# A chunked delta rule on TensorE: products of the next chunk issued in turn with those of this one

## The chip, the cores and the metric

The kernel runs on one core of a Trainium2 chip. The metric is the device time of one execution in microseconds (us). Before the change the median of three runs is 3013.03 us (3005.29 to 3014.2).

Matrix products run on TensorE (PE in the profile), elementwise work on VectorE (DVE) and ScalarE (ACT), which also empty the banks that TensorE writes. TensorE works its instructions off in the order in which the program lists them.

## What is computed

A trunk of two layers over 1024 tokens of width 1024. In each layer two kinds of recurrent heads run beside each other, then a gated feed-forward block and a gated embedding add. The change lies in the odd layer, in the heads of the delta rule, 8 heads of 64 by 64 state each:

```python
def step(state, xs):                                   # _rwkv7_scan, one token
    r_t, w_t, k_t, v_t, kk_t, a_t = xs
    sa = jnp.einsum("bhij,bhj->bhi", state, -kk_t)
    state = (state * w_t[:, :, None, :] + sa[..., None] * (kk_t * a_t)[:, :, None, :]
             + v_t[..., None] * k_t[:, :, None, :])
    return state, jnp.einsum("bhij,bhj->bhi", state, r_t)
```

The kernel does not step token by token. It takes 64 tokens (a chunk) at once, with one triangular inverse for each head and chunk, and only the state goes from chunk to chunk.

## The kernel before

**Two kinds of work share TensorE.** The dense products (all projections, feed-forward and gates) write banks named `acc`: each weight block and each operand is split into a high and a low part (`whi`, `wlo`, `xhi`, `xlo`, `ghi`, `glo`), and three products of 512 columns replace one. There are some 10,700 of them. The mixers' products write banks named `mx`, drawn by `bank()` from a pool of four. They are plain float32, and the profile counts each of them as two passes (transposes as one). A scheduler that sees a number for each instruction (`at`, `tick`, `lagging`) puts the mixers' products between the dense ones, so that dense products fill the time in which a mixer waits for ScalarE or VectorE.

**The delta rule.** `r7_unit` works on 256 tokens, four times in all (u = 0 to 3), each with four chunks of 64 (c = 0 to 3). In order:

- The two small projections (`lora` in the names): rows 0 to 63 of the array for the first, 64 to 127 for the second, four banks, emptied by ScalarE.
- `r7_scores`, for all four chunks: products of `ar` and `bk` for the even heads on rows 0 to 63, for the odd heads on rows 64 to 127, a bank each. VectorE masks each bank into `pm`.
- `r7_inverse`: a triangular inverse on VectorE and some 32 by 32 products; its result is `tt`.
- `r7_chunk`, chunk after chunk. Per chunk: four transposes of `bk` (L199), copied by ScalarE into `bt` (L1041); four products of `v` with the constant `cen`, the **values**, on columns 0 to 63 of the array, copied into the low half of `vu` (L1046); one bank that takes, for each pair of heads in turn, a product of the state `r_S` with `ar` (the **received** part, 128 rows by columns 64 to 127) and two products of `pm` with the values (the **open** part, 64 rows by 64 columns), copied into `r` (L1057); eight products of `tt` with `r` (the **solved** part, rows and columns 64 to 127), copied into the high half of `vu` (L1063); one bank for the output, again in turn one state product on the full array and two of `pm` with `vu` on column halves, copied into `o` (`keepC`, L1070); eight products of `bt` with `vu` on alternate column halves, from which VectorE makes the new state.

A row such as `128*64` in the profile gives the rows and columns of the array that a product uses. In the names `w` stands for `vu`, `r` or `bt`, which share a pool, and `sm` for `v`.

Of the kernel before, what the change touches and what calls it, by code (L numbers as in the profile page):

```python
# [10 lines left out]
F32 = mybir.dt.float32  # L11
# [8 lines left out]
P = 128  # L20
# [7 lines left out]
W2 = 7  # L28
# [80 lines left out]
class Trunk:  # L109
# [82 lines left out]
    def mm(self, out, lhsT, rhs, start=True, stop=True):  # L192
        with self.lagging():
            self.nc.tensor.matmul(out, lhsT, rhs, start=start, stop=stop)  # L194
        self.tick()

# [726 lines left out]
    def r7_unit(self, z, u, mixed):  # L923
        nc = self.nc
# [11 lines left out]
        for rows, bias, dst in ((slice(0, 64), self.w0h, w1), (slice(64, P), self.a0h, ta)):  # L936
            for jj in range(2):
                ps = self.bank()
                for j in (2 * jj, 2 * jj + 1):
                    self.mm(ps[:, UNIT * (j % 2):UNIT * (j % 2 + 1)], self.lora[rows, P * j:P * j + P], wag[rows, 0])  # L940
                for j in (2 * jj, 2 * jj + 1):
                    self.act(dst[:, j], ps[:, UNIT * (j % 2):UNIT * (j % 2 + 1)], AF.Tanh,
                             bias=bias[:, j:j + 1], scale=0.5)
# [77 lines left out]
    def r7_scores(self, c, ar, bk):  # L1021
        C = 64
        pm = self.work.tile([P, 2, 4, P], F32, tag="w4", bufs=W4, name=self.name("pm"))
        for par in range(2):
            rows = slice(C * par, C * par + C)
            ps = self.bank()
            for j in range(4):
                self.mm(ps[:, P * j:P * j + P], bk[rows, j, c], ar[rows, j, c])
            self.mul(pm[:, par], ps.rearrange("p (j t) -> p j t", j=4),
                     self.rmask.unsqueeze(1).broadcast_to([P, 4, P]))  # L1030
        return pm

    def r7_chunk(self, c, ar, bk, v, gs, o, pm, tinv, first):

        nc = self.nc
# [5 lines left out]
        nc.scalar.copy(bt, ps.rearrange("p (j t) -> p j t", j=4))  # L1041
        vu = self.work.tile([P, 8, C], F32, tag="w2", bufs=W2, name=self.name("w2_"))
        ps = self.bank()
        for j in range(4):
            self.mm(ps[0:C, P * j:P * j + P], v[:, j, C * c:C * c + C], self.cen)
        nc.scalar.copy(vu[0:C], ps[0:C].rearrange("p (h e) -> p h e", h=8))  # L1046
        hi = slice(C, P)
        S = self.r7_S[self.r7_i]
        ps = self.bank()
        for j in range(4):  # L1050
            if not first:
                self.mm(ps[hi, P * j:P * j + P], ar[:, j, c, 0], S[:, j], True, False)
            for par in range(2):
                h = 2 * j + par
                self.mm(ps[hi, C * h:C * h + C], pm[0:C, par, j, 0:C], vu[0:C, h], first, first or par == 1)
        r = self.work.tile([P, 8, C], F32, tag="w2", bufs=W2, name=self.name("w2_"))
        nc.scalar.copy(r[hi], ps[hi].rearrange("p (h e) -> p h e", h=8))  # L1057
        ps = self.bank()
        for j in range(4):
            for par in range(2):  # L1060
                h = 2 * j + par
                self.mm(ps[hi, C * h:C * h + C], tinv[:, 4 * par + j], r[hi, h])
        nc.scalar.copy(vu[hi], ps[hi].rearrange("p (h e) -> p h e", h=8))  # L1063
        ps = self.bank()
        for j in range(4):
            if not first:
                self.mm(ps[:, C * j:C * j + C], S[:, j], ar[:, j, c, 1], True, False)
            for par in range(2):
                self.mm(ps[C * par:C * par + C, C * j:C * j + C], vu[:, 2 * j + par], pm[:, par, j, C:P], first, True)
        nc.scalar.copy(o[:, :, C * c:C * c + C], ps[:, 0:4 * C].rearrange("p (j t) -> p j t", j=4))  # L1070
        ps = self.bank()
        for j in range(4):
            for par in range(2):
                self.mm(ps[C * par:C * par + C, C * j:C * j + C], bt[:, j, C * par:C * par + C], vu[:, 2 * j + par])
        pv = ps[:, 0:4 * C].rearrange("p (j e) -> p j e", j=4)
        self.r7_i ^= 1
        S2 = self.r7_S[self.r7_i]
        t = self.work.tile([P, 4, C], F32, tag="w1", bufs=2, name=self.name("w1_"))
        for par in range(2):
            rows = slice(C * par, C * par + C)  # L1080
            self.add(t[rows], pv[rows], S[rows, :, rows])
            self.mul(S2[rows, :, rows], t[rows], gs[rows, :, c:c + 1].broadcast_to([C, 4, C]))

# [403 lines left out]
```

## Time and profile before

| | |
|---|---|
| median of the runs | 3013.03 us |
| the profiled execution | 3014.3 us |
| its span, first to last instruction | 3012.6 us |
| PE busy | 2937.0 us, 97% |
| DVE busy | 1958.8 us, 65% |
| ACT busy | 1253.9 us, 42% |
| DMA, mean rate | 119 GB/s |

Matrix products are pipelined: one lasts longer than the distance to the next. What a product costs is read from the distance between the starts of neighbouring rows, not from its duration.

### The profile page before, as it was taken

How to read it: one execution, taken by the hardware profiler on the slowest of the kernel's cores; microseconds unless marked ns; L12 is line 12 of the kernel's file. 1: busy time of each engine (PE TensorE's matmuls, PEld its weight loads, DVE VectorE, ACT ScalarE, POOL GpSimd, SP SyncE). 2: the span in 40 equal slices, each digit the busy share in tenths (PEclk: the TensorE clock that was granted, in tenths of full speed). 3: DMA queues.
4: the chain of work that ended last, by engine and by line, in shares of the span. 5: the costliest groups of instructions: out<-in, count | busy, mean ns of one | idle time of the engine just before them, and what ended most of it. 6: DMA issues, size and time to landing. Idle time of an engine off the chain costs nothing.

```text
span 3012.6 us, 38754 instructions
## 1 busy us (share of the span) xinstructions
PE 2937.0 (97%) x15102; PEld 2381.2 (79%) x15102; DVE 1958.8 (65%) x3313; ACT 1253.9 (42%) x1783; POOL 28.0 (1%) x97
## 2 busy tenths in 40 slices
PE   8999989999999999999999999999999999999997
PEld 6877768878878887877877778787878777888886
DVE  7566655756687557836787584684787497555457
ACT  5354554333244536224444443542453454322224
POOL 0000010000000000000000000000000000000000
PEclk9999989999999999999999999999999999999999
DMA  5443553333245554422333444532333135333333
GB/s 198 143 156 104 186 200 98 107 88 105 81 118 168 168 166 128 104 66 91 102 102 102 133 141 143 161 95 67 91 116 98 51 96 170 98 119 98 98 91 105
DMA packets 197287, 357.79 MB, mean 119 GB/s; under 512 B 64848, under 2 KB 100816, under 8 KB 197104
## 3 DMA queue, kind: packets, MB, share of 16 engines
q1 hardware_dynamic: 197104, 355.33, 38.7%
q8 instruction: 118, 1.93, 0.3%
q14 instruction: 65, 0.53, 0.1%
HBM read 298.61 MB, written 56.66 MB: 118 GB/s over the span
## 4 chain that ended last, share of the span: by engine, by line
PE 84%; DVE 9%; ACT 3%; issue 2%; DMA 1%; POOL 0%; SPq 0%; DVEq 0%; ACTq 0%; POOLq 0%
PE acc L194 71%; PE mx L194 13%; DVE wlo L168 2%; DVE w L181 1%; DVE w L168 1%; DVE tmp L168 1%; PE mx L199 1%; ACT w L189 1%; ACT whi L332 1%; DVE cols L168 1%; ACT L189 0%; DVE h L181 0%; DVE tmp L181 0%; DVE w L789 0%; DMA h<-in_x_dram 0%
## 5 line engine op out<-in xcount | busy, mean ns | idle before, releaser
L194 PE MATMUL acc<-xhi,whi 128*128 128x512 f32 x2864 | 1140.5, 399 | 11.8 <-ACT whi L332 8.8
L194 PE MATMUL acc<-xlo,whi 128*128 128x512 f32 x2864 | 1131.3, 396 | 4.2 <-DVE xlo L168 3.3
L194 PE MATMUL acc<-xhi,wlo 128*128 128x512 f32 x2864 | 1128.1, 394 | 2.7 <-DVE wlo L168 2.6
L332 ACT CAST whi<-wraw 128x1024 fp32r<-128x1024 f32 (+1 forms) x450 | 463.6, 1030 | 1158.9 <-PE acc L194 834.8
L194 PEld LDWEIGHTS acc<-xhi,whi 128*128 128x128 f32 x2864 | 540.2, 189 | 132.1 <-ACT whi L332 9.8
L194 PEld LDWEIGHTS acc<-xlo,whi 128*128 128x128 f32 x2864 | 540.1, 189 | 123.5 <-DVE xlo L168 7.2
L194 PEld LDWEIGHTS acc<-xhi,wlo 128*128 128x128 f32 x2864 | 539.4, 188 | 123.8 <-DVE wlo L168 6.0
L168 DVE TENSOR_TENSOR wlo<-wraw,whi 128x1024 fp32r<-128x1024 f32 (+1 forms) x450 | 539.0, 1198 | 102.8 <-ACT whi L332 101.7
L168 DVE TENSOR_TENSOR tmp<-acc,rs 128x512 f32<-128x512 f32 (+1 forms) x205 | 140.8, 689 | 354.4 <-PE acc L194 354.0
L194 PE MATMUL acc<-ghi,whi 128*128 128x512 f32 x704 | 277.6, 396 | 1.0 <-ACT ghi L332 1.0
L194 PE MATMUL acc<-glo,whi 128*128 128x512 f32 x704 | 275.0, 391 | 0.0
L194 PE MATMUL acc<-ghi,wlo 128*128 128x512 f32 x704 | 275.0, 391 | 0.0
L168 DVE TENSOR_TENSOR tmp<-tmp,acc 128x512 f32<-128x512 f32 x88 | 60.4, 686 | 166.1 <-PE acc L194 165.7
L189 ACT ACTIVATE w<-w 128x1024 f32<-128x1024 f32 (+2 forms) x124 | 113.3, 920 | 113.0 <-DVE w L168 53.3
L194 PEld LDWEIGHTS acc<-ghi,whi 128*128 128x128 f32 x704 | 131.9, 188 | 29.8 <-ACT ghi L332 1.9
L194 PEld LDWEIGHTS acc<-ghi,wlo 128*128 128x128 f32 x704 | 132.1, 188 | 27.9 <-issue 0.3
L194 PEld LDWEIGHTS acc<-glo,whi 128*128 128x128 f32 x704 | 132.2, 188 | 27.2 <-DVE glo L168 0.6
L181 DVE SCALAR_TENSOR_TENSOR h<-acc,h 128x512 f32<-128x512 f32 x144 | 98.7, 687 | 63.0 <-PE acc L194 62.4
L189 ACT ACT_TABLE_LOAD x84 | 107.8, 1283 | 10.3 <-DMA h<-in_x_dram 4.7
L181 DVE SCALAR_TENSOR_TENSOR tmp<-tmp,tmp 128x512 f32<-128x512 f32 x120 | 82.2, 686 | 12.7 <-ACT tmp L189 12.6
L189 ACT ACTIVATE tmp<-tmp 128x512 f32<-128x512 f32 x120 | 75.4, 629 | 28.9 <-DVE tmp L168 28.0
L181 DVE SCALAR_TENSOR_TENSOR w<-zin,cols,w 128x256 f32<-128x256 f32 x192 | 82.5, 479 | 5.5 <-ACT w L189 5.2
(296 smaller groups left out, 2603.8 us busy)
## 6 DMA issues: line engine op xcount, KB each, us to landing
wraw<-in_ffn_w_gate_dram SPq DMA_DIRECT2D x88, 512.0 KB, 3.6
wraw<-in_ffn_w_up_dram SPq DMA_DIRECT2D x88, 512.0 KB, 3.6
wraw<-in_ffn_w_down_dram SPq DMA_DIRECT2D x64, 512.0 KB, 3.6
wraw<-in_o_w_in_dram SPq DMA_DIRECT2D x60, 512.0 KB, 3.6
wraw<-in_e_w_in_dram SPq DMA_DIRECT2D x48, 512.0 KB, 3.7
wraw<-in_ple_w_gate_dram SPq DMA_DIRECT2D x32, 512.0 KB, 3.7
wraw<-in_ffn_w_down_dram SPq DMA_DIRECT2D x32, 384.0 KB, 3.1
up<-tmp SPq DMA_DIRECT2D x32, 256.0 KB, 2.3
```

The lines of the kernel that those rows point to most:

```text
L168: (eng or self.nc.vector).tensor_tensor(out, a, b, op=op)
L181: self.nc.vector.scalar_tensor_tensor(out, a, s, b, op0=op0, op1=op1)
L189: self.nc.scalar.activation(out, a, f, **kw)
L194: self.nc.tensor.matmul(out, lhsT, rhs, start=start, stop=stop)
L199: self.nc.tensor.transpose(out, a, self.ident)
L332: self.nc.scalar.copy(hi, src)
```

## The change

Nothing is added to or taken from the computation: both programs have the same 15,102 passes on TensorE. What changes is their order and which of them share a bank.

- `together` runs several lists of products side by side, one product of each in turn, and keeps that order on TensorE.
- The two small projections and the scores are issued with the two row halves in turn.
- The values and the open part of a chunk no longer stand in that chunk. Those of chunk 0 are issued ahead of the loop; those of chunk c + 1 are issued inside chunk c. The values of c + 1 (columns 0 to 63) go in turn with the received part of c (columns 64 to 127), the open part of c + 1 (rows 0 to 63) in turn with the solved part of c (rows 64 to 127).
- The open part starts the bank; the received part of the next chunk adds to it and ends it. That bank is held meanwhile.
- In the output bank the four state products come first, then the eight of `pm`.

```diff
+    def together(self, *products):
+        with self.tc.manual_schedule(engines={mybir.EngineType.PE}):
+            for _ in zip_longest(*products):
+                pass
...
+        vu = self.vu()
+        self.together(self.r7_values(0, v, vu))
+        ps = self.bank()
+        self.together(self.r7_open(ps, pms[0], vu, u == 0))
         for c in range(4):
             tc = tinv[c // 2][64:P, 8 * (c % 2):8 * (c % 2) + 8]
-            self.r7_chunk(c, ar, bk, v, gs, o, pms[c], tc, u == 0 and c == 0)
+            ps, vu = self.r7_chunk(c, ar, bk, v, gs, o, pms, tc, ps, vu, u == 0 and c == 0)
...
+    def r7_values(self, c, v, vu):
+        C = 64
         ps = self.bank()
         for j in range(4):
-            self.tr(ps[:, P * j:P * j + P], bk[:, j, c].rearrange("p i t -> p (i t)"))
+            self.mm(ps[0:C, P * j:P * j + P], v[:, j, C * c:C * c + C], self.cen)
+            yield
+        self.nc.scalar.copy(vu[0:C], ps[0:C].rearrange("p (h e) -> p h e", h=8))
+
+    def r7_open(self, ps, pm, vu, alone=False):
+        C = 64
+        for h in range(8):
+            j, par = divmod(h, 2)
+            self.mm(ps[C:P, C * h:C * h + C], pm[0:C, par, j, 0:C], vu[0:C, h], h == 0, alone and h == 7)
+            yield
...
-        for j in range(4):
-            if not first:
-                self.mm(ps[hi, P * j:P * j + P], ar[:, j, c, 0], S[:, j], True, False)
-            for par in range(2):
-                h = 2 * j + par
-                self.mm(ps[hi, C * h:C * h + C], pm[0:C, par, j, 0:C], vu[0:C, h], first, first or par == 1)
...
+        def received():
+            for j in range(4):
+                if not first:
+                    self.mm(ps[hi, P * j:P * j + P], ar[:, j, c, 0], S[:, j], False, j == 3)
+                yield
+            nc.scalar.copy(r[hi], ps[hi].rearrange("p (h e) -> p h e", h=8))
+        self.together(received(), *(() if last else (self.r7_values(c + 1, v, nvu),)))
+
+        def solved(sums):
+            for h, (j, par) in enumerate(heads):
+                self.mm(sums[hi, C * h:C * h + C], tinv[:, 4 * par + j], r[hi, h])
+                yield
+            nc.scalar.copy(vu[hi], sums[hi].rearrange("p (h e) -> p h e", h=8))
+        sums = self.bank()
+        nps = None if last else self.bank()
+        self.together(*(() if last else (self.r7_open(nps, pms[c + 1], nvu),)), solved(sums))
+        sums = self.bank()
+        if not first:
+            for j in range(4):
+                self.mm(sums[:, C * j:C * j + C], S[:, j], ar[:, j, c, 1], j == 0, False)
+        for h, (j, par) in enumerate(heads):
+            self.mm(sums[C * par:C * par + C, C * j:C * j + C], vu[:, h], pm[:, par, j, C:P], first and j == 0, j == 3)
```

**First place: TensorE, unit u = 2, chunk 0, from the received part to the solved part.** Before (`mx_15466` is the bank that received and open part share, `w_2710` is `vu`):

```order
L194 MATMUL mx_15466<-w_2710_15459,pm_15228 64x64 x2
L194 MATMUL mx_15466<-r_S_9213,ar_15096 64x128
L194 MATMUL mx_15466<-w_2710_15459,pm_15228 64x64 x2
L194 MATMUL acc_17857<-xhi_17232,whi_17853 128x512
L194 MATMUL acc_17857<-xlo_17233,whi_17853 128x512
L194 MATMUL acc_17857<-xhi_17232,wlo_17854 128x512
L194 MATMUL acc_17857<-xhi_17236,whi_17853 128x512
L194 MATMUL mx_15481<-w_2713_15479,tt_15370 64x64 x8
```

After, the same place (the received part fills `mx_15522`, the values of chunk 1 fill `mx_15546`; `mx_15558` is chunk 1's open part, `mx_15557` chunk 0's solved part):

```order
L194 MATMUL mx_15522<-r_S_9213,ar_15156 64x128
L194 MATMUL mx_15546<-cen,sm_15250 64x128
L194 MATMUL acc_17977<-xlo_17353,whi_17973 128x512
L194 MATMUL acc_17977<-xhi_17352,wlo_17974 128x512
L194 MATMUL acc_17977<-xhi_17356,whi_17973 128x512
L194 MATMUL acc_17977<-xlo_17357,whi_17973 128x512
L194 MATMUL acc_17977<-xhi_17356,wlo_17974 128x512
L194 MATMUL mx_15558<-w_2714_15542,pm_15301 64x64
L194 MATMUL mx_15557<-w_2713_15541,tt_15430 64x64
```

The first two rows are the last of four such pairs, the last two the first of eight. The group in which state and `pm` products took turns is gone; its halves stand beside the values and the solved part of another chunk.

**Second place: TensorE, the same chunk, the output bank.** Before (`mx_15491`):

```order
L194 MATMUL mx_15491<-pm_15228,w_2710_15459 64x64 x2
L194 MATMUL mx_15491<-ar_15096,r_S_9213 128x64
L194 MATMUL mx_15491<-pm_15228,w_2710_15459 64x64 x2
L194 MATMUL mx_15505<-w_2710_15459,w_2709_15457 64x64 x8
L199 MATMUL mx_15519<-ident,bk_15097 128x128 x4
```

After (`mx_15579`):

```order
L194 MATMUL mx_15579<-ar_15156,r_S_9213 128x64 x4
L194 MATMUL acc_17977<-xhi_17360,whi_17973 128x512
L194 MATMUL mx_15579<-pm_15288,w_2708_15512 64x64 x8
L194 MATMUL mx_15593<-w_2708_15512,w_2712_15539 64x64 x8
L205 MATMUL mx_15607<-ident,bk_15157 128x128 x4
```

The four state products moved into one row ahead of the eight others.

**Third place: ScalarE, the copies of the same chunk.** Before (values, received and open, solved, output):

```order
L1046 COPY w_2710_15459<-mx_15460 64x512
L1057 COPY w_2713_15479<-mx_15466 64x512
L1063 COPY w_2710_15459<-mx_15481 64x512
L1070 COPY keepC_15226<-mx_15491 128x4x64
L1041 COPY w_2719_15524<-mx_15519 128x512
```

After (received and open, values of chunk 1, solved, output, next transposes):

```order
L1089 COPY w_2713_15541<-mx_15522 64x512
L1057 COPY w_2714_15542<-mx_15546 64x512
L1096 COPY w_2708_15512<-mx_15557 64x512
L1106 COPY keepC_15286<-mx_15579 128x4x64
L1079 COPY w_2722_15612<-mx_15607 128x512
```

The copy of the values now follows right behind that of the received part, and the pair of open and solved products stands behind both.

## Rows read from the trace of the kernel before

**Rows 1.** The page: engines' busy time, granted clock, chain by engine

```profile
PE 2937.0 (97%) x15102; PEld 2381.2 (79%) x15102; DVE 1958.8 (65%) x3313; ACT 1253.9 (42%) x1783; POOL 28.0 (1%) x97
...
PE 84%; DVE 9%; ACT 3%; issue 2%; DMA 1%; POOL 0%; SPq 0%; DVEq 0%; ACTq 0%; POOLq 0%
```

**Rows 2.** Busy time by stretch: length, PE, PEld, DVE, ACT, POOL, clock, DMA, GB/s

```profile
2066.00:2124.00 58.00, 58.00 (x479) 42.27 (x476) 14.51 (x25) 18.21 (x29) 0.68 (x3) 1.00 0.10 29
...
2404.00:2497.00 93.00, 86.64 (x458) 71.62 (x456) 84.36 (x129) 50.72 (x65) 0.00 (x0) 0.98 0.39 126
```

**Rows 3.** Timeline, TensorE, u = 2, chunk 0: start, length, form, passes

```profile
2067.25 0.76 PE L194 MATMUL mx<-cen,sm 128*64 128x128 f32 x5
2067.74 0.32 PE L194 MATMUL mx<-r_S,ar 128*64 128x128 f32 x1
2067.84 0.27 PE L194 MATMUL mx<-cen,sm 128*64 128x128 f32 x1
...
2068.26 0.50 PE L194 MATMUL acc<-xhi,whi 128*128 128x512 f32 x1
...
2069.16 0.44 PE L194 MATMUL mx<-w,pm 64*64 64x64 f32 x4
...
2071.36 0.44 PE L194 MATMUL mx<-w,pm 64*64 64x64 f32 x4
2071.73 0.50 PE L194 MATMUL acc<-xhi,whi 128*128 128x512 f32 x1
2072.07 0.40 PE L194 MATMUL acc<-xlo,whi 128*128 128x512 f32 x1
...
2072.53 0.40 PE L194 MATMUL acc<-xhi,whi 128*128 128x512 f32 x1
2072.86 1.14 PE L194 MATMUL mx<-w,tt 64*64 64x64 f32 x16
2073.93 0.43 PE L194 MATMUL mx<-ar,r_S 128*128 128x64 f32 x2
...
2075.32 0.43 PE L194 MATMUL mx<-ar,r_S 128*128 128x64 f32 x2
2075.68 0.34 PE L194 MATMUL mx<-pm,w 128*64 128x64 f32 x4
...
2076.94 0.34 PE L194 MATMUL mx<-pm,w 128*64 128x64 f32 x4
2077.11 0.64 PE L194 MATMUL mx<-w,w 128*64 128x64 f32 x16
2077.68 0.66 PE L199 MATMUL mx<-ident,bk 128*128 128x128 f32 x4
```

**Rows 4.** Timeline, TensorE: full-array products of 64 columns in one row

```profile
2436.82 1.89 PE L194 MATMUL mx<-w 128*128 128x64 f32 x16
2438.53 0.48 PE L194 MATMUL acc<-xhi,wlo 128*128 128x512 f32 x1
```

**Rows 5.** Timeline, TensorE: small projections of u = 0 and of u = 1

```profile
1126.86 2.96 PE L194 MATMUL mx<-sm,lora 64*128 64x256 f32 x16
1130.28 0.50 PE L194 MATMUL acc<-xhi,whi 128*128 128x512 f32 x1 [0.46 <-ACT xhi L332]
...
1506.70 2.00 PE L194 MATMUL mx<-sm,lora 64*128 64x256 f32 x12
```

**Rows 6.** Timeline, TensorE and VectorE: scores of u = 1 and their masking

```profile
1563.16 5.04 PE L194 MATMUL mx<-ar,bk 64*128 64x128 f32 x64
...
1564.35 4.88 DVE L168 TENSOR_TENSOR pm<-mx,rmask 128x512 f32<-128x512 f32 x8 [1.05 <-PE mx L194]
```

**Rows 7.** Timeline, ScalarE and VectorE, u = 2, chunk 0 into chunk 1

```profile
2068.37 0.58 ACT L1046 COPY w<-mx 64x512 f32<-64x512 f32 x1 [0.41 <-PE mx L194]
...
2079.87 1.04 ACT L332 CAST whi<-wraw 128x1024 fp32r<-128x1024 f32 x1
...
2078.70 0.87 DVE L168 TENSOR_TENSOR r_S<-w,gs 64x256 f32<-64x256 f32 x2
```

More of the change, by code (lines that the diff above doesn't have):

```diff
@@ L2 @@
 from contextlib import ExitStack, contextmanager
-from itertools import chain
+from itertools import chain, zip_longest
 import concourse.bass as bass
@@ L935, in r7_unit @@
         w1, ta = self.w4(), self.w4()
[L936 to L939, printed above, removed]
+        parts = ((slice(0, 64), self.w0h, w1), (slice(64, P), self.a0h, ta))
+        for jj in range(2):
+            pss = [self.bank() for _ in parts]
+            for j in (2 * jj, 2 * jj + 1):
+                for ps, (rows, _, _) in zip(pss, parts):
                     self.mm(ps[:, UNIT * (j % 2):UNIT * (j % 2 + 1)], self.lora[rows, P * j:P * j + P], wag[rows, 0])
+            for ps, (_, bias, dst) in zip(pss, parts):
                 for j in (2 * jj, 2 * jj + 1):
@@ L1023, in r7_scores @@
         pm = self.work.tile([P, 2, 4, P], F32, tag="w4", bufs=W4, name=self.name("pm"))
-        for par in range(2):
-            rows = slice(C * par, C * par + C)
-            ps = self.bank()
-            for j in range(4):
+        pss = [self.bank() for _ in range(2)]
+        for j in range(4):
+            for par, ps in enumerate(pss):
+                rows = slice(C * par, C * par + C)
                 self.mm(ps[:, P * j:P * j + P], bk[rows, j, c], ar[rows, j, c])
+        for par, ps in enumerate(pss):
             self.mul(pm[:, par], ps.rearrange("p (j t) -> p j t", j=4),
@@ L1031, in r7_scores, with vu @@
         return pm
-    def r7_chunk(self, c, ar, bk, v, gs, o, pm, tinv, first):
-        nc = self.nc
+    def vu(self):
+        return self.work.tile([P, 8, 64], F32, tag="w2", bufs=W2, name=self.name("w2_"))
+    def r7_values(self, c, v, vu):
         C = 64
@@ L1038, in r7_chunk @@
         for j in range(4):
-            self.tr(ps[:, P * j:P * j + P], bk[:, j, c].rearrange("p i t -> p (i t)"))
-        bt = self.w2()
[L1041 to L1050, printed above, removed]
-            if not first:
-                self.mm(ps[hi, P * j:P * j + P], ar[:, j, c, 0], S[:, j], True, False)
-            for par in range(2):
-                h = 2 * j + par
-                self.mm(ps[hi, C * h:C * h + C], pm[0:C, par, j, 0:C], vu[0:C, h], first, first or par == 1)
-        r = self.work.tile([P, 8, C], F32, tag="w2", bufs=W2, name=self.name("w2_"))
-        nc.scalar.copy(r[hi], ps[hi].rearrange("p (h e) -> p h e", h=8))
@@ L1058, in r7_chunk @@
[L1058 to L1075, printed above, removed]
+            self.mm(ps[0:C, P * j:P * j + P], v[:, j, C * c:C * c + C], self.cen)
+            yield
+        self.nc.scalar.copy(vu[0:C], ps[0:C].rearrange("p (h e) -> p h e", h=8))
@@ new lines, in r7_open, with r7_chunk @@
+    def r7_open(self, ps, pm, vu, alone=False):
[4 more added lines that the diff above has]
+            yield
+    def r7_chunk(self, c, ar, bk, v, gs, o, pms, tinv, ps, vu, first):
+        nc = self.nc
+        C = 64
+        hi = slice(C, P)
+        pm, S = pms[c], self.r7_S[self.r7_i]
+        heads = [divmod(h, 2) for h in range(8)]
+        sums = self.bank()
+        for j in range(4):
+            self.tr(sums[:, P * j:P * j + P], bk[:, j, c].rearrange("p i t -> p (i t)"))
+        bt = self.w2()
+        nc.scalar.copy(bt, sums.rearrange("p (j t) -> p j t", j=4))
+        r = self.vu()
+        last = c == 3
+        nvu = None if last else self.vu()
+        def received():
+            for j in range(4):
+                if not first:
[11 more added lines that the diff above has]
+        self.together(*(() if last else (self.r7_open(nps, pms[c + 1], nvu),)), solved(sums))
+        sums = self.bank()
+        if not first:
+            for j in range(4):
+                self.mm(sums[:, C * j:C * j + C], S[:, j], ar[:, j, c, 1], j == 0, False)
+        for h, (j, par) in enumerate(heads):
+            self.mm(sums[C * par:C * par + C, C * j:C * j + C], vu[:, h], pm[:, par, j, C:P], first and j == 0, j == 3)
+        nc.scalar.copy(o[:, :, C * c:C * c + C], sums[:, 0:4 * C].rearrange("p (j t) -> p j t", j=4))
+        sums = self.bank()
+        for h, (j, par) in enumerate(heads):
+            self.mm(sums[C * par:C * par + C, C * j:C * j + C], bt[:, j, C * par:C * par + C], vu[:, h])
+        pv = sums[:, 0:4 * C].rearrange("p (j e) -> p j e", j=4)
@@ L1082, in r7_chunk @@
             self.mul(S2[rows, :, rows], t[rows], gs[rows, :, c:c + 1].broadcast_to([C, 4, C]))
+        return nps, nvu
     def fetch(self, hf, spare=False):
```

## The prediction

> **What bounds the kernel now.** I read the page first: TensorE is busy 97% of the span and carries 84% of the chain that ended last [rows 1]. A busy share alone says little of a pipelined engine, so I went on to the stretches in which the changed code runs. In the chunk loop of u = 2 TensorE is busy for all of 58.00 us, while VectorE works 14.51 us and ScalarE 18.21 us [rows 2]. Nothing waits there: TensorE has more in its list than it can issue, and a product that takes less room in the list moves everything behind it forward. So the question is how much room each form takes, and I read that from the distances between starts in the timeline of one chunk [rows 3].
>
> Three things can be seen there. First, products of one form and one position follow each other at a steady distance: the `tt` group has 16 passes in 1.07 us (2072.86 to 2073.93). Second, a change of form costs extra: a dense product keeps a distance of 0.23 us (2072.07 to 2072.53 is two), but the one before a mixer group has 0.33 us (2072.53 to 2072.86) and the first one after a group 0.34 us (2071.73 to 2072.07). Third, products on different column halves run at the same time: a pass of `r_S` on columns 64 to 127 starts at 2067.74 while `cen` passes on columns 0 to 63 still start at 2067.84, and the 16 `w,w` passes on alternate halves take 0.57 us (2077.11 to 2077.68) where the 16 passes of `tt`, all on one position, take 1.07 us.
>
> **The change, part by part.** All sums are made against the profiled execution, 3014.3 us (span 3012.6 us and 1.7 us around it).
>
> *The chunk before.* Values: 2067.25 to 2068.26, 1.01 us. Received and open part in turn: from the first to the fourth `pm` group, 2069.16 to 2071.36, are three periods, so 0.73 us a period and 2.93 us for four; the `pm` half of one is 0.37 us (2071.36 to 2071.73), the state's half 0.36 us. Solved: 1.07 us. Output bank: a period of 0.63 us (2075.68 to 2076.94 is two), four make 2.52 us. Together 7.53 us of issue [rows 3]. Transposes and the `bt` products stay as they are.
>
> *The chunk after.* The received part is four products like the values, on the other column half; the pair is counted as one of them, 1.01 us. The open part is eight products like the solved ones, on the other row half; the pair is counted as 1.07 us. In the output bank the four state products come in a row: 0.36 us for one with the change of form (2075.32 to 2075.68 [rows 3]) and six more passes at 0.107 us, the distance in a row of 16 such passes (1.71 us [rows 4]): 1.00 us. The eight `pm` products on alternate halves are counted like the `w,w` row, 0.57 us. Together 3.65 us, so 3.88 us less for each chunk.
>
> *Over the four units.* Three units (u = 1 to 3) had 4 x 7.53 = 30.1 us. They now have the values and open part of chunk 0 alone, 1.01 + 1.07 = 2.08 us, and 4 x 3.65 = 14.6 us (chunk 3 has its received and solved part without a partner, at the same price). That saves 13.4 us each, 40.3 us. Unit 0 has no state in chunk 0: before 1.01 + 1.07 + 1.07 + 0.57 = 3.72 us and three full chunks, 26.3 us; after 2.08 us, then 1.01 + 1.07 + 0.57 = 2.65 us, then three at 3.65 us, 15.7 us. It saves 10.6 us. Sum 50.9 us. Two corrections: in seven places before, the order puts the first received product directly behind the values, where it already runs beside them, so 7 x 0.36 = 2.5 us were not there to save. And the order has 80 stretches of mixer products in these loops instead of 93; a round trip costs 0.10 + 0.11 us on the dense side (0.33 and 0.34 against 0.23) and about somewhat less on the mixer side (a first pair of passes that takes longer and a longer way out), estimated at 0.36 us in all, so 13 of them are 4.7 us. The chunk loops save 50.9 - 2.5 + 4.7 = 53.1 us.
>
> *The two small projections.* In u = 1 twelve passes take 2.00 us, four of them overlapped with four others: eight places [rows 5]. In turn all 16 passes fit in eight places, 2.00 us, where u = 0 takes 2.96 us [rows 5]. That is 0.96 us in u = 0, 2 and 3 and 0.86 us in u = 1, 3.7 us at most. But in u = 0 the next dense product waits 0.46 us for ScalarE's `xhi` anyway [rows 5], and u = 2 shows the same wait; there I count nothing. 1.8 us remain.
>
> *The scores.* I count nothing. The 64 passes take 5.04 us, and VectorE masks the eight banks in 4.88 us without a gap from 1564.35 on [rows 6]; with four banks in the pool, the fifth to eighth bank wait for it. The row halves already overlap where one bank follows the other. In turn, a pair of banks ends later than the first of them does now, so VectorE starts no earlier. The Trainium skill has the rule (TensorEngine Tiling (Array Packing), PSUM Bottleneck) that tiling speeds up TensorE but not the emptying of its banks; the trace agrees here, with 4.88 us of masking under 5.04 us of products. Without that bound, 32 paired places at 0.112 us (estimated from the pitch of one-position products of 128 columns, 1.01 us for eight passes less the change of form) would take some 3.6 us and give 1.4 us a unit, 5.6 us in all; the other end is a loss of 0.3 us a unit.
>
> *New waits.* The pair of open and solved products waits for two copies instead of one. The copy of the values starts 0.11 us after the dense product that follows them (2068.26 [rows 3] to 2068.37) and takes 0.58 us [rows 7]; two copies are ready 1.27 us after that dense product starts. The order puts five dense products there: 0.34, 3 x 0.23 and 0.33 us, 1.36 us. That just covers. Behind the waiting pair are queued all dense products, and the next chunk's state. If a weight cast (1.04 us [rows 7]) sits ahead of the copies, up to 1.04 us a chunk are lost, 16.6 us in 16 chunks; at the other end nothing. The casts are few in this stretch (ScalarE is 31% busy, most of it with these copies), so I take 3 us, near the lower end. The other joints keep their cover: the copy after the solved part has four state products and a dense one ahead of the products that need it (about 1.3 us against 0.11 + 0.58 = 0.69 us), and the new state, ready at 2079.57 (2078.70 + 0.87 us [rows 7]), 1.89 us after the transposes start at 2077.68, has these (0.6 us) and six to nine dense products (1.4 to 2.1 us) as cover.
>
> Sum: 53.1 + 1.8 + 0 - 3 = 51.9 us, 2962.4 us against the profiled 3014.3. That execution lies 1.3 us above the median of the runs, so the **forecast is 2961 us**.
>
> **The rivals.**
>
> *The pairs do not run at the same time.* The open and solved products lie on different rows but write the same 64 columns' output, which no row of the chunk shows. If they queue, twelve open parts cost 1.07 us each, 12.8 us; if the received part and the values queue too, twelve times 1.01 us, 12.1 us: 2974 or 2986 us. Against it speak the overlap of the column halves [rows 3] and of the row halves in the small projections, where 12 passes take 2.00 us [rows 5]. The Trainium skill (TensorE: Matmul & The Clock Gate, Part 3: Packing small matmuls) says that a weight load overlaps running products only when the row group differs; by that rule the column pair would queue. The trace disagrees for `cen` and `r_S` at 2067.74. Chance 0.10.
>
> *The double copy is late.* Every chunk meets a cast in front of its copies: 2961 + 16.6 - 3 = 2975 us. For it: the cover is only as long as the copies. Against: few casts. Chance 0.12.
>
> *The gain is given back behind the loop.* In the stretch 2404 to 2497 VectorE works 84.36 of 93 us [rows 2], and the HGRN2 products there stand elsewhere in the new order. If half of the saving turns into waits for VectorE, 2961 + 26 = 2987 us; all of it would be no change. Against: VectorE is three quarters idle in the loop itself, so little of its work was done under the time that goes. Chance 0.09, of which 0.04 within 0.3%.
>
> *Slower: the chain of the chunk takes over.* From received part to received part the chain is 1.01 + 1.27 (two copies) + 1.07 + 0.69 + 1.14 (output and `bt`, 0.57 us each) + 1.89 = 7.1 us, and TensorE has about 9.5 us of work in a chunk after (3.65, transposes and `bt` 1.2, some 20 dense products 4.6). If each of its three stops at ScalarE met a cast and an activation (1.04 and 0.63 us) and the state's stop at VectorE a `wlo` and another operation (some 1.9 us), the chain would grow by 6.9 us, 4.5 us over TensorE's work: 16 x 4.5 = 72 us, 3033 us. It decides from 3.8 us lost per chunk, (52 + 9)/16. Against it: 29 instructions of ScalarE and 25 of VectorE in the whole loop of u = 2 [rows 2]. Chance 0.03.
>
> **How the numbers follow.** The forecast itself has 0.66. A measurement of this kernel tells about 0.3% from no change, 9 us, so faster means below 3004 us: 0.66 + 0.10 + 0.12 + 0.05 = 0.93; same 0.04; slower 0.03. The range goes up to both pairs queueing, 2986 us. Downward it takes no waits (3 us), the rest of the projections (1.9 us), the scores (5.6 us) and some of the spread of the runs: 2949 us. Below and above it I leave about 0.18.
>
> **What would show it.** In the trace after: `r_S` and `cen` passes in turn that take about 1.0 us for 16, `pm` and `tt` in turn about 1.1 us for 32 passes; four `ar,r_S` products in about 1.0 us; a chunk loop of u = 2 some 14 us shorter with TensorE still busy throughout; 64 score passes still at about 5 us. Wrong would be: 32 passes in 2.1 us (no overlap of rows), idle time in front of `mx` products put down to L1057 or L1089, or a loop that is shorter while the stretch behind it is longer by as much.

## The result, and the profile after

The changed kernel takes 2963.27 us (median of 4 runs, 2959.74 to 2965.94), against 3009.61 us for the kernel before (4 runs). The ratio is 0.9851, with a 95% interval of 0.9838 to 0.9863: 1.5% faster. The forecast was 2961 us in a range of 2949 to 2987. The profiled execution of the changed kernel lasts 2963.97 us, its span is 2962.3 us.

The page of the changed kernel gives busy time by engine, and the chain that ended last by engine:

```profile
PE 2880.3 (97%) x15102; PEld 2348.6 (79%) x15102; DVE 1958.8 (66%) x3313; ACT 1256.0 (42%) x1784; POOL 27.8 (1%) x97
...
PE 83%; DVE 10%; ACT 2%; issue 2%; DMA 2%; POOL 0%; SPq 0%; DVEq 0%; ACTq 0%; POOLq 0%
```

TensorE does the same 15,102 passes and is as full as before [rows 1], 97%; its busy time fell by 56.7 us. So the products take less room, and TensorE still bounds the kernel. By stretch, the chunk loop of u = 2 and the stage behind the last loop (columns as in [rows 2]):

```profile
2041.00:2086.00 45.00, 45.00 (x487) 35.32 (x487) 14.65 (x25) 18.27 (x29) 0.65 (x2) 1.00 0.13 40
2352.00:2450.00 98.00, 88.72 (x464) 73.76 (x463) 86.64 (x132) 54.97 (x69) 0.00 (x0) 0.95 0.38 120
```

The loop fits in 45 us with about the same passes, where 58 us stood before, and TensorE is busy for all of it. The second line is a stage in which VectorE is nearly full; it will matter below. The timeline of TensorE, u = 2, chunk 0, shows the two pairs and the output bank (start, length, form, passes):

```profile
2045.84 0.32 PE L194 MATMUL mx<-r_S,ar 128*64 128x128 f32 x1
2045.85 0.32 PE L194 MATMUL mx<-cen,sm 128*64 128x128 f32 x1
2046.00 0.27 PE L194 MATMUL mx<-r_S,ar 128*64 128x128 f32 x1
2046.01 0.27 PE L194 MATMUL mx<-cen,sm 128*64 128x128 f32 x1
...
2046.86 0.50 PE L194 MATMUL acc<-xlo,whi 128*128 128x512 f32 x1
...
2047.90 0.39 PE L194 MATMUL acc<-xhi,wlo 128*128 128x512 f32 x1
2048.22 0.32 PE L194 MATMUL mx<-w,pm 64*64 64x64 f32 x2
2048.42 0.24 PE L194 MATMUL mx<-w,tt 64*64 64x64 f32 x1
2048.42 0.27 PE L194 MATMUL mx<-w,pm 64*64 64x64 f32 x1
2048.49 0.22 PE L194 MATMUL mx<-w,tt 64*64 64x64 f32 x1
...
2049.46 1.10 PE L194 MATMUL mx<-ar,r_S 128*128 128x64 f32 x8
2050.37 0.47 PE L194 MATMUL acc<-xhi,whi 128*128 128x512 f32 x1
2050.78 0.69 PE L194 MATMUL mx<-pm,w 128*64 128x64 f32 x16
2051.29 0.64 PE L194 MATMUL mx<-w,w 128*64 128x64 f32 x16
...
2056.95 0.27 PE L194 MATMUL mx<-w,pm 64*64 64x64 f32 x1
2056.96 0.27 PE L194 MATMUL mx<-w,tt 64*64 64x64 f32 x1
```

The last two rows are the start of the row pair of chunk 1. Received part and values start 0.01 us apart, and the 16 passes take 1.02 us (2045.84 to 2046.86), as long as the eight passes of the values alone took before [rows 3]. Open and solved part take 1.24 us for 32 passes (2048.22 to 2049.46): the second lane starts one product late, 0.20 us, after that the two keep step. This is not so in every chunk: in chunk 1 the lanes start 0.01 us apart and the pair takes 1.08 us. Of the seven row pairs that stand in one piece, five take 1.24 to 1.26 us and two 1.08 us; why was not found out. The state's products of the output take 0.91 us and the `pm` products 0.51 us. The four numbers add to 3.68 us for chunk 0. The copies on ScalarE that the second pair waits for:

```profile
2046.96 0.58 ACT L1089 COPY w<-mx 64x512 f32<-64x512 f32 x1 [0.43 <-PE mx L194]
2047.57 0.58 ACT L1057 COPY w<-mx 64x512 f32<-64x512 f32 x1
```

The second copy ends at 2048.15, the pair starts at 2048.22, at the usual distance behind the last dense product. The cover holds by 0.07 us here, and no wait of TensorE on L1089 or L1057 stands in the list of waits of the whole execution.

**Where the time went.** Between the starts of the same two dense products, ahead of a loop and behind its last `bt` product, the two executions compare as follows (us, after less before): chunk loops of u = 0 to 3: -9.3, -13.9, -13.3 and -13.4, together **-50.0**; small projections -2.3 in all; scores +0.3 in all; the stage behind the last loop +0.9.

The same distances are used for the experiments, because the first 1124 us, whose order is the same in all kernels here, differ by up to 13.5 us from one execution to another. Part of that shows as a lower granted clock in the stretch from 200 to 300 us, here in the kernel before and then in e11 (the column behind POOL is the granted clock):

```profile
200.00:300.00 100.00, 98.34 (x557) 77.76 (x556) 61.88 (x139) 43.73 (x82) 1.04 (x6) 0.90 0.41 129
```

```profile
200.00:300.00 100.00, 98.89 (x598) 80.17 (x597) 64.50 (x148) 46.84 (x86) 1.04 (x6) 1.00 0.45 137
```

In the same 100 us, the one with the granted clock of 0.90 issues 557 passes, the other 598. The total of one execution therefore tells some 10 us at best. A loop tells tenths as long as the clock holds: it is 1.00 in the four loops of the kernel before and of the changed one. Behind the loop of u = 1 it is not: the 150 dense products there (1718 to 1765 us in the changed kernel) take 47.7 us at a granted clock of 0.96, in e2 48.9 us at 0.93 and in e4 46.0 us at 1.00, with the same two waits of 1.4 to 1.5 us. So the marks stand directly behind the loops.

### The profile page after: what moved, and what is told of

Read it like the earlier page. It is cut to its first block, busy times and chain, and to the rows that moved or that the text cites. A ratio compares the mean times of both kernels' runs of the same rounds, so it can differ in the third digit from the quotient of the medians.

```text
span 2962.3 us, 38752 instructions
## 1 busy us (share of the span) xinstructions
PE 2880.3 (97%) x15102; PEld 2348.6 (79%) x15102; DVE 1958.8 (66%) x3313; ACT 1256.0 (42%) x1784; POOL 27.8 (1%) x97
## 4 chain that ended last, share of the span: by engine, by line
PE 83%; DVE 10%; issue 2%; ACT 2%; DMA 2%; POOL 0%; SPq 0%; DVEq 0%; ACTq 0%; POOLq 0%
PE acc L194 71%; PE mx L194 11%; DVE wlo L168 2%; DVE w L181 1%; DVE w L168 1%; DVE tmp L168 1%; PE mx L205 1%; ACT w L189 1%; DVE cols L168 1%; ACT whi L338 1%; ACT L189 0%; DVE tmp L181 0%; DMA zin<-z_k 0%; DMA w<-invt 0%; DMA tmp<-mixed 0%
```

## The experiments

Theory: the time goes because (a) products of one form stand in a row instead of in turn, (b) products on free rows or columns run at the same time, and (c) nothing new is waited for. Rival to (b): the products of a pair queue, and the gain is all (a) and the chunk ahead. A table of all runs (each ratio is against runs of the kernel before on the same chip, whose medians lie from 3007.76 to 3010.61 us); "loops" is the sum of the four loops less that of the kernel before (for e10 between marks further behind, since there products that follow a loop move into it), "behind" the length of the stage behind the last loop.

| kernel | median, us | ratio, 95% interval | loops | behind |
|---|---|---|---|---|
| before | 3009.61 | | 0 | 232.5 |
| after | 2963.27 | 0.9838 to 0.9863 | -50.0 | 233.4 |
| e1_rows_listed | 2967.55 | 0.9841 to 0.9887 | -41.8 | 234.4 |
| e2_columns_listed | 2967.33 | 0.9835 to 0.9876 | -44.6 | 235.0 |
| e3_grouped_only | 2975.66 | 0.9874 to 0.9905 | -26.9 | 228.4 |
| e4_output_alternating | 2977.23 | 0.9874 to 0.9908 | -39.0 | 240.0 |
| e5_groups_unbroken | 2943.46 | 0.9768 to 0.9800 | see below | 226.2 |
| e6_scores_two_engines | 2962.92 | 0.9831 to 0.9869 | -50.0 | 236.6 |
| e7_unbroken_two_engines | 2947.82 | 0.9765 to 0.9812 | see below | 226.2 |
| e8_both_listed | 2975.89 | 0.9875 to 0.9907 | -35.4 | 234.3 |
| e9_unbroken_same_due | 2959.26 | 0.9822 to 0.9856 | see below | see below |
| e10_due_earlier | 2976.08 | 0.9870 to 0.9911 | -34.0 | 234.1 |
| e11_projections_scores_only | 3006.32 | 0.9979 to 1.0004 | -0.5 | 232.7 |

**The row pair as two lists.** First all open products, then all solved ones; the rest as in the changed kernel.

```diff
-        self.together(*(() if last else (self.r7_open(nps, pms[c + 1], nvu),)), solved(sums))
+        self.together(chain(*(() if last else (self.r7_open(nps, pms[c + 1], nvu),)), solved(sums)))
```

> The changed kernel, but the open products of chunk c + 1 and the solved ones of chunk c are issued as two lists, eight and then eight, instead of in turn; nothing else moves. Theory (two array halves run at once only while their products are neighbours in the list): the 32 passes take about 2.0 us instead of 1.2 us in each of twelve chunks, with some overlap at the seam; 7 to 10 us slower than the changed kernel, about 2971 us, ratio to the kernel before 0.987 to 0.989. Rival (TensorE finds partners wherever they stand in its queue, so the order within the pair does nothing): the 32 passes still take 1.2 us, 2963 us, ratio 0.985.

The loops are 8.1 us longer than in the changed kernel. The timeline of this kernel, same place:

```profile
2047.44 0.97 PE L194 MATMUL mx<-w,pm 64*64 64x64 f32 x13
2048.20 0.27 PE L194 MATMUL mx<-w,tt 64*64 64x64 f32 x1
2048.25 0.22 PE L194 MATMUL mx<-w,pm 64*64 64x64 f32 x1
...
2048.42 0.92 PE L194 MATMUL mx<-w,tt 64*64 64x64 f32 x13
2049.27 1.10 PE L194 MATMUL mx<-ar,r_S 128*128 128x64 f32 x8
```

The 32 passes take 1.83 us instead of 1.24. Only the last three passes of the first list overlap with the first three of the second. TensorE does start a product ahead of ones listed before it (here the order is not strictly that of the list, as the opening has it), but only a few passes ahead: the list has to bring the partners together. Seven of the twelve pairs stand in one piece in both kernels, all of u = 2 and u = 3 among them; there the pairs take 1.83 us each where they took 1.08 to 1.26, 4.4 us in all. In u = 2 that is the whole of the 1.9 us by which the loop is longer. The other 3.7 us lie in u = 0 and u = 1, where dense products stand inside the pairs. The rival to (b) falls for the rows.

**The column pair as two lists.** All received products, then all values of the next chunk.

```diff
-        self.together(received(), *(() if last else (self.r7_values(c + 1, v, nvu),)))
+        self.together(chain(received(), *(() if last else (self.r7_values(c + 1, v, nvu),))))
```

> The changed kernel, but the received products of chunk c and the values of chunk c + 1 are issued as two lists, four and then four. Theory (neighbours only): the 16 passes take 1.5 to 1.8 us instead of 1.0 us in twelve chunks; 5 to 9 us slower than the changed kernel, about 2970 us, ratio 0.987 to 0.988. Rival (partners are found anywhere in the queue): 1.0 us, 2963 us, ratio 0.985.

The loops are 5.4 us longer. In the trace five `r_S` passes stand alone, then three pairs overlap, then five `cen` passes stand alone: 1.51 us where the pair takes 1.02, in eight places that stand in one piece, 3.9 us of the 5.4. The loops are as expected; the totals of this run and the last can't be told from the changed kernel's, for the reason above.

**Both pairs as lists.** The chunk ahead stays, both alternations go.

> The changed kernel with both pairs written as lists: all eight received products, then all values of the next chunk; all open products of the next chunk, then all solved ones. The chunk ahead stays, the alternation goes. One list alone cost the loops 8.2 us (open and solved) and 5.4 us (received and values). If the two pairs are independent, the loops are 13.6 us longer than in the changed kernel, a gain of 36.4 us over the kernel before instead of 50.0, total about 2977 us. Rival: in a row of four lists the last products of one run beside the first of the next at every seam, and the losses don't add; then the loops are 8 to 10 us longer, total about 2972 us.

The loops are 14.5 us longer, 1 us more than the sum of 8.1 and 5.4: the losses of the two pairs add, and the rival (8 to 10 us) falls.

**Grouping alone.** The kernel before, with one edit: in the bank of received and open part, and in the output bank, the state's products come first and those of `pm` behind them. No chunk ahead, no pairs.

```diff
-        for j in range(4):
-            if not first:
-                self.mm(ps[hi, P * j:P * j + P], ar[:, j, c, 0], S[:, j], True, False)
-            for par in range(2):
-                h = 2 * j + par
-                self.mm(ps[hi, C * h:C * h + C], pm[0:C, par, j, 0:C], vu[0:C, h], first, first or par == 1)
+        if not first:
+            for j in range(4):
+                self.mm(ps[hi, P * j:P * j + P], ar[:, j, c, 0], S[:, j], j == 0, False)
+        for h in range(8):
+            j, par = divmod(h, 2)
+            self.mm(ps[hi, C * h:C * h + C], pm[0:C, par, j, 0:C], vu[0:C, h], first and h == 0, h == 7)
```

(and the same in the output bank)

> The kernel before, with one part of the change: in the bank of the received and open part, and in the output bank, the four state products come first and the eight others behind them. Nothing is issued a chunk ahead, nothing in turn. Theory (what counts is room in TensorE's list, and about half of the saving is the changes of form between neighbours): some 28 to 30 us saved, about 2980 us, ratio 0.990 to 0.991. Rival (the saving is the work that was moved a chunk ahead of its waits): nothing saved, 3009 us, ratio 1.000. Second rival (all of it is products running at once): 0 to 5 us saved, ratio 0.998 to 1.000.

The loops are 26.9 us shorter than before, and the stage behind the last one is 4.1 us shorter. Its timeline has the groups one by one:

```profile
2052.28 1.10 PE L194 MATMUL mx<-ar,r_S 128*128 128x64 f32 x8
...
2056.95 1.09 PE L194 MATMUL mx<-r_S,ar 128*64 128x128 f32 x8
...
2058.40 1.14 PE L194 MATMUL mx<-w,pm 64*64 64x64 f32 x16
```

So over half of the gain of the loops needs neither the chunk ahead nor two products at a time: it is what TensorE loses when small products of different forms take turns [rows 3]. The division of the 50.0 us is then: grouping 26.9, the chunk ahead as lists 8.5 more (35.4 with both lists), the alternation 14.5 on top. What makes up the 8.5 us (three passes that still overlap at each seam, and eleven stretches of these products fewer than in e3) was not told apart.

**The output bank as before.** The changed kernel, but in the output bank state and `pm` products in turn.

> The changed kernel with the output bank in the order of before: one state product on the full array, two on column halves, four times. Theory (each change of form costs): 0.95 us more in each of fifteen chunks and some split groups, 14 to 17 us slower than the changed kernel, about 2978 us, ratio 0.989 to 0.991. Rival (the same passes take the same room in any order): 2963 us, ratio 0.985.

The total is 14 us longer, as expected, but not for that reason alone: the loops are only 11.0 us longer, and the stage behind them 6.6 us. Where the bank alternates the period is 0.63 us as before; but in the first chunk of u = 2 the scheduler puts three dense products behind the first state product, so that one change of form there serves a dense stretch as well. The loops of u = 2 and u = 3 lose 0.9 us a chunk, those of u = 0 and u = 1, where more dense products stand between, 0.6 us: the 0.95 us of the prediction is the upper end here.

**Projections and scores alone.** The kernel before with only these two in turn.

> The kernel before with only the changed order of the small projections and of the scores; the chunk loops are as before. By the prediction's sum and the rows of the changed kernel: projections 2.3 us shorter in all (0.9 each in the units u=1 and u=3, next to nothing in u=0 and u=2), scores 0 to 0.4 us longer each; total about 3008 us, not to be told from the kernel before. Rival: the scores do run at once on the two halves as soon as the neighbouring code is that of before; then the 64 passes fall from 5.0 to 3.7 us, 5 us in all, and the total is about 3002 us.

The ratio is 0.9991 (0.9979 to 1.0004): no change. The scores change by -0.04, +0.35 and -0.04 us in u = 0 to 2. The rival (scores run at once) falls.

**Scores with two engines to empty the banks.** The changed kernel; ScalarE copies the odd heads' banks and GpSimd masks them in memory.

```diff
-        for par, ps in enumerate(pss):
-            self.mul(pm[:, par], ps.rearrange("p (j t) -> p j t", j=4),
-                     self.rmask.unsqueeze(1).broadcast_to([P, 4, P]))
+        mask = self.rmask.unsqueeze(1).broadcast_to([P, 4, P])
+        pvs = [ps.rearrange("p (j t) -> p j t", j=4) for ps in pss]
+        self.nc.scalar.copy(pm[:, 1], pvs[1])
+        self.mul(pm[:, 0], pvs[0], mask)
+        self.mul(pm[:, 1], pm[:, 1], mask, eng=self.nc.gpsimd)
```

> The changed kernel, except that the odd heads' score bank is emptied by ScalarE (a plain copy to memory) and masked there by GpSimd, while the even heads' bank is masked by VectorE as before. The prediction put the 64 passes of scores at no gain, since VectorE empties their banks at 4.9 us for eight and TensorE waits for them. By that theory two engines that empty banks let the 64 passes fall from about 5.0 us towards 3.7 us (32 passes took 2.06 us where no bank was waited for, so 64 take about 4.1), 0.9 to 1.3 us in each of the four units, 4 to 5 us in all: about 2959 us. Rival: the passes themselves set the 5.0 us (they don't run at once on the two halves); then the 64 passes stay at 5.0 us, and the total at 2963 us, or above it if GpSimd's masking makes the first chunk wait.

First the scores of u = 1 in the changed kernel, TensorE and VectorE, then in this one:

```profile
1553.47 2.06 PE L194 MATMUL mx<-ar,bk 64*128 64x128 f32 x32
1555.17 4.87 DVE L168 TENSOR_TENSOR pm<-mx,rmask 128x512 f32<-128x512 f32 x8
...
1555.90 2.95 PE L194 MATMUL mx<-ar,bk 64*128 64x128 f32 x32 [0.38 <-DVE pm L168]
```

```profile
1556.08 4.49 PE L194 MATMUL mx<-ar,bk 64*128 64x128 f32 x64
...
1558.04 5.00 POOL L168 TENSOR_TENSOR pm<-pm,rmask 128x512 f32<-128x512 f32 x4 [183.10 <-ACT pm L1043]
```

The first 32 passes, with free banks, take 2.06 us; the second 32 wait for VectorE and take 2.95 us. With two engines all 64 take 4.49 us instead of 5.38, and each unit's scores are 0.9 us shorter. The banks were the bound, as the prediction said. But the total is the same. The loops themselves are as long as in the changed kernel to within 0.1 us. Behind those of u = 0 and u = 1 TensorE waits longer for VectorE (0.92 us instead of 0.23 for `keepC` in u = 0, 2.5 us instead of 1.4 for `wlo` in u = 1). The stage behind the last loop is 3.2 us longer with nearly the same waits (12.3 us against 12.5) and a lower granted clock (0.96 against 0.98).

**Groups in one piece.** The changed kernel, but no dense product is put inside a pair, nor inside the output and `bt` groups. A group's products get one due time, and what follows comes 8 steps later (the products of the output stand under the same `whole()`, not shown).

```diff
+    @contextmanager
+    def whole(self):
+        step, self.step = self.step, 0
+        yield
+        self.step = step
+        self.tc.cur_priority += 8 * step
...
-        with self.tc.manual_schedule(engines={mybir.EngineType.PE}):
+        with self.whole(), self.tc.manual_schedule(engines={mybir.EngineType.PE}):
...
+        with self.whole():
             for h, (j, par) in enumerate(heads):
                 self.mm(sums[C * par:C * par + C, C * j:C * j + C], bt[:, j, C * par:C * par + C], vu[:, h])
```

> The changed kernel, except that no dense product is put inside a group any more: the two alternating pairs, the eight products that add the state's and the chunk's share of the output, and the eight products that advance the state are each issued in one piece, and the dense products that stood between them follow behind. The theory of the sum (a change from 128-wide products to small ones and back costs about 0.36 us, wherever it is) expects a gain: the order of the instructions has about 15 fewer such stretches over the four chunk loops than the changed kernel's, 15 x 0.36 = 5.4 us, and within the loops up to 6.4 us less than after; total about 2957 us (2954 to 2961). Rival: the dense products put between were also what bridged TensorE's waits for the copies of VectorE and ScalarE; with the groups in one piece the copies come late, TensorE waits 0.5 to 1 us in each of the 12 chunks, and the loops are the same or up to 6 us longer than in the changed kernel (2963 to 2969).

2943.46 us: the fastest kernel here, 2.2% under the kernel before and some 20 us under the changed one, where 5.4 were expected. In the traces the loops of u = 0 to 3 are 4.4, 1.8, 1.8 and 0.0 us shorter than in the changed kernel (u = 2 with the projection behind it, which is issued inside the loop here), 8.0 in all, and the stage behind the last loop is 7.2 us shorter. Another 7.8 us of the difference between the two profiled executions lie ahead of the first loop, where the code is the same: they are no gain of the edit. Waits of TensorE in the first 98 us of that stage, in the changed kernel and in this one (sum in us, times, longest):

```profile
PE acc L194 <- DVE tmp L168: 3.7, 1, 3.7
PE mx L194 <- DVE keepC L181: 2.7, 1, 2.7
PE mx L205 <- DVE keepB L168: 2.7, 1, 2.7
```

```profile
PE mx L194 <- ACT w L892: 1.0, 1, 1.0
PE mx L194 <- DVE keepC L181: 0.5, 1, 0.5
PE mx L212 <- DVE keepB L168: 0.5, 1, 0.5
PE mx L194 <- DVE w L168: 0.3, 1, 0.3
```

Waits of 9.1 us became 2.3 us, and over the whole stage 12.5 us became 5.2 us, which is the 7.2 us to within a tenth; the granted clock over the whole stage is 0.98 in both. The price of a stretch explains the loops only in part (15 fewer at 0.36 us are 5.4 us of 8.0), and the last stage not at all. Both edits at once, this one and the two engines, add nothing:

> The two edits together: groups in one piece, and the scores' banks emptied by two engines. If both theories hold and the gains lie in different stretches, they add: 5 to 6 us from the loops and 4 to 5 us from the scores, about 2952 us (2949 to 2957). If the waits for the copies take the first gain back, it is about 2959 us; if neither holds, 2963 us or more.

2947.82 us, with an interval that covers the run before it. The scores are 0.9, 0.7 and 0.9 us shorter in u = 0 to 2 than in the changed kernel, and it is not seen in the total. Against e6, which has the scores of this kernel and the groups of the changed one, it is 15.1 us faster: the 8.0 and 7.2 us again.

**The two halves of that edit.** Groups in one piece with the due times of the changed kernel:

> The kernel with groups in one piece gained about 20 us over the changed kernel where 5.4 were expected; in its trace about 7.5 us of that lie in the four chunk loops, 7.2 us in the stage behind the last loop (226.2 us against 233.4), and some 8 us ahead of the first loop, where the code is the same. Its edit did two things: no dense product inside a group, and the due times of what follows a group were earlier (8 steps for a pair of 16 products). This kernel does the first alone: groups in one piece, due times as in the changed kernel. If the two are what they seem, the loops are 6 to 8 us shorter than the changed kernel's, and the stage behind the last loop is as long as there (232 to 234 us); total about 2956 us (2951 to 2960). Rival: the groups in one piece also end the waits of the last stage, by leaving more dense products for it; then it takes 226 us, and the total is about 2949 us.

The loops of u = 0 to 2 are 3.9, 1.4 and 0.8 us shorter than in the changed kernel, with 8, 3 and 2 stretches fewer: 6.0 us for 13, 0.46 us a stretch where the prediction has 0.36. Behind each of the loops of u = 1 and u = 2, up to the next projection, 1.0 us is lost again. But from the last projection to the end of the last stage it takes 392.3 us where the changed kernel takes 387.6 and the kernel with earlier due times 380.9. The expectation for the last stage was wrong, and so was its rival.

Earlier due times with dense products still allowed inside (`whole()` stands around the same products):

```diff
+    @contextmanager
+    def whole(self):
+        due = self.tc.cur_priority
+        yield
+        self.tc.cur_priority = due + 8 * self.step
```

> The changed kernel with the due times of what follows a group as early as in the kernel with groups in one piece, but with the dense products still put inside the groups. If the gain of the last stage comes from the due times, the stage behind the last loop takes about 226 us and the loops are as long as in the changed kernel (within 2 us in all): total about 2956 us. Rival: it comes from the groups in one piece; then the stage takes 232 to 234 us, and the total is about 2963 us.

The loops are 16.1 us longer than in the changed kernel, which neither theory expected. The timeline shows why (u = 2, chunk 0):

```profile
2051.20 0.43 PE L194 MATMUL mx<-ar,r_S 128*128 128x64 f32 x2
2051.57 0.33 PE L194 MATMUL mx<-w,pm 64*64 64x64 f32 x2
2051.82 0.43 PE L194 MATMUL mx<-ar,r_S 128*128 128x64 f32 x2
2052.19 0.33 PE L194 MATMUL mx<-w,tt 64*64 64x64 f32 x2
2052.44 0.43 PE L194 MATMUL mx<-ar,r_S 128*128 128x64 f32 x2
```

The state's products of the output now come due inside the pair, and each turn from the full array to a 64 by 64 product and back costs 0.62 us. In the order they stand in 48 stretches instead of 16; 32 turns at 0.41 us (0.62 less two passes of 0.107 us) are 13 of the 16 us. In two places inside these loops the granted clock is 0.57 (1334 to 1338 and 2075 to 2079 us), where the changed kernel's loops run at 1.00. It is the loss of the kernel before, in another place. Neither half of the edit gives the last stage its 226 us: one shows 234.1, the other's last unit is longer as a whole. That stage ran from 226 to 240 us over these kernels, which compute the same there. Its waits are mostly for VectorE; which instruction decides them stays open.

## Why the prediction was right

- **What bounds the kernel.** TensorE's list, and within it the room that each form takes: confirmed. TensorE stays busy for all of the loop, and the loop shrinks by what its products' distances say.
- **The chunk after.** Predicted 1.01 + 1.07 + 1.00 + 0.57 = 3.65 us; measured in chunk 0 of u = 2 1.02 + 1.24 + 0.91 + 0.51 = 3.68 us. The row pair was sized too low by 0.17 us (the late second lane), the output too high by 0.15 us; that the two errors cancel is luck. In chunk 1 the lanes are not late, and the pair takes 1.08 us as sized.
- **The loops.** 53.1 us, less 3 for waits, is 50.1; measured 50.0. But no wait of that kind appeared, so the 53.1 was too high by 3 us, and the agreement to a tenth is luck. The distances from each start to the next, added up by form over the four loops of both traces, say where. Values, received, open and solved parts saved 32.3 us where the sum has 34.2: after the change they take 45.1 us instead of 41.6, 2.5 of the 3.5 us in u = 0 and u = 1, where dense products split the pairs, which the chunk of u = 2 that was priced does not show; in the kernel before they took 1.6 us more than the sum, so the correction of 2.5 us for parts that already overlapped was too large. The output bank saved 12.7 us where the sum has 14.2: its four turns of 0.63 us count too much of the kernel before (2.31 us in the chunk shown, not 2.52), since the first state product is cut off from the rest by dense products and the last `pm` passes make room after 0.17 us [rows 3]. All else (dense products beside a group 2.8, transposes 1.7, `bt` products 0.5) saved 5.0 us, where the term of the 13 fewer stretches has 4.7. The price of a stretch came out somewhat higher in e9, 0.46 us instead of 0.36.
- **The projections.** 1.8 us predicted, 2.3 measured (0.3, 0.9, 0.1 and 1.0 in u = 0 to 3): the two units that wait for ScalarE anyway gained nearly nothing, as said; in u = 0 the wait for `xhi` grew from 0.46 to 1.29 us.
- **The scores.** 0 predicted, +0.3 measured; the bound by bank emptying is shown by e6. The Trainium skill's rule (TensorEngine Tiling (Array Packing), PSUM Bottleneck), that tiling does not speed up the emptying of banks, agrees with it.
- **Pairs that queue.** The runs with lists rule it out: with the partners apart the loops are 8.1 and 5.4 us longer. The bound for it, 12.8 and 12.1 us, was too high, since at the seam of two lists three passes overlap all the same.
- **The Trainium skill's rule on weight loads** (TensorE: Matmul & The Clock Gate, Part 3: Packing small matmuls), overlap only on different row groups, does not hold here: `r_S` and `cen` both use all 128 rows, and their passes, weight loads included, start 0.01 us apart (loads at 2046.00 and 2046.01 while earlier passes of both run).
- **A late double copy.** It did not happen, though with 0.07 us to spare in the chunk shown.
- **Gain given back behind the loop.** +0.9 us in the profiled execution, so nearly none; but the stage moves by 14 us with the order, and e4 and e6 lost 6.6 and 3.2 us there, e6 at a lower granted clock. The rival was better founded than its chance suggests: the trace of before could not show which way that stage would fall.
- **What the prediction did not say.** It gave the whole saving to pairs and groups without dividing it. The grouping, which needs none of the new machinery, is 27 of the 50 us.

## What to carry to other kernels

Read what a small product costs from the distances between starts, and look first for places where products of different shape take turns: putting equal ones in a row is the cheaper half of such a gain. Products on disjoint rows or columns run at once, but only if the list has the partners within a few passes of each other. When a scheduler places by due times, look at the order that comes out, since a group that is spread too thin or made due too early is broken up by others, and judge an edit by distances between the same instructions, where totals scatter by 10 us, and look at the granted clock between them.

## What the runs showed of the hardware

- Two products on different column halves, both 128 rows deep, start 0.01 us apart; 16 passes of 128 columns take 1.02 us, as eight alone do.
- A product can start ahead of products listed before it when its part of the array is free, but only some three passes ahead: of two lists with 16 passes each, three overlapped.
- Of seven row pairs in one piece, the second lane started 0.20 to 0.22 us late in five (1.24 to 1.26 us a pair) and 0.01 us late in two (1.08 us).
- A turn from the full array to a 64 by 64 tile and back cost about 0.41 us, also when all of it is small products; at a granted clock of 1.00, the level of 2.4 GHz.
- The same code ran at granted clocks of 0.90 to 1.00 in the stretch from 200 to 300 us, and with the rest of the scatter ahead of the first loop this moved whole executions by up to 13.5 us.
- The same 150 dense products behind the loop of u = 1 (e4, the changed kernel and e2), with the same two waits, took 46.0 us at a granted clock of 1.00, 47.7 us at 0.96 and 48.9 us at 0.93.
